# Four projection banks until the first scores, z:0 ahead of the first merge, and rk behind the second

## The chip, the cores and the metric

One core of a Trainium2 chip runs one launch of the kernel. The metric is the device time of the launch in microseconds (us). Engines: PE is TensorE, ACT ScalarE, DVE VectorE, POOL GpSimd, and SP is SyncE, whose queue issues every DMA of this kernel.

## The reference

Two post-norm decoder layers on a 256 x 1024 residual stream, float32. Each has one input projection for two head groups, an output projection, a norm, a gated MLP with a short convolution, and a second norm.

```python
def hybrid_layer(x, ...):
    proj = x @ w_in
    q_a, k_a, v_a, a_logit, b_logit, z, q_b, k_b, v_b = jnp.split(proj, offs, -1)
    o_a = gdn_mixer(q_a, k_a, v_a, a_logit, b_logit, z, ...)
    o_b = moba_mixer(q_b, k_b, v_b, pos)
    mix = jnp.concatenate([o_a, o_b], -1) @ w_out
    x = layer_norm(DEEPNORM_ALPHA * x + mix, ln1_g, ln1_b)
    ...
```

`gdn_mixer` is a gated delta rule with 4 heads of 128 and chunks of 64: q, k and v pass a causal convolution of four taps and silu, q and k are normalised, and for each chunk a unit lower triangular system (64 x 64, `a_strict` plus identity) is solved; its output is multiplied by silu(z). `moba_mixer` is block attention with 8 heads of 64; with 256 tokens it is one causal block.

## The kernel before, in words

Sequence is on the free axis: a projection chunk gives 128 output features x 256 tokens. A weight chunk is loaded in float32 by SP (`load_raw`, L181, tile wr, 6 buffers), split into a rounded part wh (ACT, L196) and a rest wl (DVE or POOL, L197), each in two halves of 512 columns and each in 5 buffers. `proj` (L204 to L214) then runs 24 matmuls of 128 x 256 into one PSUM bank: eight pairs xh·wh, xl·wh (L211, L212) and eight xh·wl (L214). The eight PSUM banks are divided (L94 to L96): pj has 2 (projections, by `ps_p`), mx 2 (scores, transposes, by `ps_m`) and ac 4 (by `ps_a`).

A layer has a mixing stage (about 20 to 160 us in layer 0, 368 to 506 us in layer 1) and an MLP stage, which the change does not touch. The mixing stage is written as units, `u_...`, that the tables `ORDER` (L72 to L87, one for a layer) list: `ka`, `va`, `qa` are the convolved projections of the delta rule (`u_conv`: projection, then ACT's L424 and DVE's three taps L427 read the bank, then tanh L429 and L430), `qb`, `kb` the rotary ones (`u_rope`), and `z` the gate (`u_z`: tanh L441 and zs L442 read the bank). `kk`, `decay`, `sk` and `am` make the triangular matrix A. `solve` inverts its 16 x 16 diagonal blocks on POOL: A goes to DRAM (da, L512), comes back as T (L518), DVE prepares it (L523), POOL runs 28 small steps (L527, L529) and a copy (L530), and the result goes to DRAM (dx, L531). `ex` reads it back (PT, L538) and DVE spreads it into gX and gx (L543). `lt` (L560) and `lx` merge 16 to 32, and `mt:32`, `mx:32`, `mt:64`, `mx:64` go on to 64. `s:p` makes attention scores of a head pair in two mx banks (L619, mask L623) and their softmax, `tr` and `pv` follow. `rk` is the inverse root of the key norms (some DVE operations on 128 x 8).

Order of work: letters behind @ in the table say on which engines the instructions of a unit are held behind those of the unit before (P is PE, A is ACT, D is DVE, G is POOL). Otherwise a scheduler places each engine's instructions by its own costs, and each engine then works them in that order. SP's queue is worked in order too: a DMA that waits holds back all behind it. In this queue the loads of layer 0's 16 weight chunks from ka:0 on stand between the masks and dx.

Of the kernel before, what the change touches and what calls it, by code (L numbers as in the profile page):

```python
# [22 lines left out]
D = 1024  # L23
S = 256
# [12 lines left out]
DP = 8 * (NB * 128 + NB)  # L37
# [33 lines left out]

ORDER = ("""  # L72
ab ka:0@A ab2@G ka:2@P qb:0@GP ka:3@G ka:1 kk:0 decay@AGD kk:1@PG kb:0@G kb:2@G sk@GP ld:0@P ld:1@DG kb:3@G am:0@A
vb:1@DAGP qb:1@GP kb:1@G rp@DG am:1@AG qb:2@G qb:3 va:2@GP va:0@G va:3 rk@G solve@G va:1@D qa:1 qa:0@P ex@DPA lt@GP s:0@DA lx@DAP
tr:0@AD mt:32:0@GAP mx:32:0@G mt:32:1@G vt:0@G rp@GP mx:32:1@PAG pv:0 mt:64:0@GDPA mt:64:1@AG s:1@AGD
qa:3@G qa:2@GP mx:64:0@PG tr:1@PA mx:64:1@D z:0 s:2@GADP pv:1@GA sq:0@DG vt:1@ADP zsol:0@D az tr:2@A s:3@GDP pv:2@AG
tr:3@PGD zsol:1@A z:2@G qk@GP sq:1@GDA o:0@ADP z:1@G wu:1@PGA pv:3@AGP o:1@GDP w:0:5 w:0:4@D w:1:4@PDA z:3@PD w:1:6@G
w:0:7@GD w:1:5@GPD ot:1@AP ot:0@G wu:0@PA w:0:6@A
""", """
vb:1@APDG ab@GD ka:0@G ab2@G ka:3 qb:0@P ka:2@G ka:1@P kk:0 decay@ADG kb:0 kk:1@GA kb:2 sk@AP kb:3@G kb:1@PG qb:2  # L80
rp@GPD qb:3@GP am:0@PA qb:1@DP am:1@AG ld:0@GP va:1@P va:0@GP rk@AG va:2@G ld:1@D solve@GP va:3@P qa:1 ex@D lt@DAP s:0@GD
lx@DAPG mt:32:0@A mt:32:1@AG vt:0@PD rp@GAD tr:0@AP qa:0 mx:32:0 pv:0@A mx:32:1@AD mt:64:0@AGD mt:64:1@DGP s:1@A
qa:3 qa:2@P mx:64:1@APD tr:1@P z:0@G s:2@G sq:0@D vt:1@DG mx:64:0@GDP pv:1 zsol:0@DGP az@A tr:2@DA s:3@GD pv:2@AG
tr:3@PDGA zsol:1@PD z:2 qk@PDG sq:1@G o:0@ADP z:1 pv:3@AGD o:1@A w:0:5@G w:0:4@DP w:1:4@GDA z:3@PA wu:0@DP w:1:6@GP
wu:1@GA w:0:7@D ot:1@D ot:0@AP w:1:5 w:0:6@PA
""")
# [3 lines left out]
def hybrid_kernel(ctx, tc, xT, x, wab, wch, par, lnrow, cst, msk, out):  # L90
# [10 lines left out]
    mx = ctx.enter_context(tc.tile_pool(name="mx", bufs=2, space=PSUM))  # L101
# [11 lines left out]
    def ps_p():  # L113
        return ps_w()[:, 0:S]

    def ps_w():
        return pj.tile([128, 512], F32, name="pj")

    def ps_m():
        return mx.tile([128, 512], F32, name="mx")  # L120
# [85 lines left out]
    def proj(ps, l, ci, le=None):  # L206
        h, lo = load_chunk(l, ci, le=le)
        h = h.rearrange("p (k m) -> p k m", k=KT)
        lo = lo.rearrange("p (k m) -> p k m", k=KT)
        for k in range(KT):  # L210
            pe.matmul(ps, h[:, k, :], xh[:, k, :], start=k == 0, stop=False)  # L211
            pe.matmul(ps, h[:, k, :], xl[:, k, :], start=False, stop=False)  # L212
        for k in range(KT):
            pe.matmul(ps, lo[:, k, :], xh[:, k, :], start=False, stop=k == KT - 1)  # L214
# [80 lines left out]
    def vb_first():  # L295
        vb = res.tile([128, 2, 512], F32, name="vb")
        ps = [ps_m() for _ in range(2)]
        for c in range(4):
            raw = wraw.tile([128, 1024], F32, name="wr")
            tiles = None  # L300
            for k in (range(2 * c, 2 * c + 2) if c == 0 else [slice(2 * c, 2 * c + 2)]):
                ks = slice(k, k + 1) if c == 0 else k
                load_x(ks)
                cs = slice(ks.start * 512 - c * 1024, ks.stop * 512 - c * 1024)
                sp.dma_start(raw[:, cs], wch[0, C_VB + c, :, cs])
                tiles = split(raw, tiles=tiles, cs=cs)
                wh, wl = tiles
                for t in range(2):
                    ts = slice(t * 128, t * 128 + 128)
                    for a, w in ((xh, wh), (xl, wh), (xh, wl)):  # L310
                        for kk in range(ks.start, ks.stop):
                            o = (kk - 2 * c) * 512
                            pe.matmul(ps[t], a[:, kk, ts], w[:, o:o + 512], start=kk == 0 and a is xh and w is wh,  # L313
                                      stop=kk == KT - 1 and w is wl)
        for t in range(2):
            act.activation(vb[:, t, :], ps[t], AF.Copy)
        return vb
# [20 lines left out]
    vb = vb_first()  # L338
    const_prep()

    for l in range(DEPTH):
# [7 lines left out]
        def sm(name):  # L349
            return small.tile(sh, F32, name=name, bufs=1)  # L350

        def mt(name, shape, bufs=1, dt=F32):
            return (early if name in EARLY else mix).tile(shape, dt, name=name, bufs=bufs)
# [5 lines left out]
        sk, cj, ncj, rk, sq, so, wv = (sm(n) for n in ("sk", "cj", "ncj", "rk", "sq", "so", "wv"))  # L359
        g_h = small.tile(sh, F32R, name="g_h", bufs=1)  # L360
        g_l = small.tile(sh, F32R, name="g_l", bufs=1)
        ka, qa = mt("ka", [128, HG, S]), mt("qa", [128, HG, S])
# [3 lines left out]
        qb, kb = mt("qb", [128, 4, S]), mt("kb", [128, 4, S])  # L366
# [8 lines left out]
        G, T, st = [], {}, {}  # L375
# [45 lines left out]
        def gdn_conv(ps, ct, dst):  # L421
            w = pr[:, P_GCONV + 4 * ct:P_GCONV + 4 * ct + 4]
            cv = mt("cv", [128, S], 2)
            act.activation(cv, ps, AF.Copy, scale=w[:, 3:4])  # L424
            for j in (2, 1, 0):
                o = 3 - j
                dve.scalar_tensor_tensor(cv[:, o:], ps[:, :S - o], w[:, j:j + 1], cv[:, o:], op0=OP.mult, op1=OP.add)  # L427
            th = mt("th", [128, S], 2)
            act.activation(th, cv, AF.Tanh, scale=0.5)  # L429
            dve.scalar_tensor_tensor(dst, th, 1.0, cv, op0=OP.add, op1=OP.mult)  # L430

        def u_conv(c0, ct, dst, h):
            ps = ps_p()
            proj(ps, l, c0 + h)
            gdn_conv(ps, ct + h, dst[:, h, :])

        def u_z(h):
            ps = ps_p()
            proj(ps, l, C_Z + h)
            th = mt("th", [128, S], 2)  # L440
            act.activation(th, ps, AF.Tanh, scale=0.5)  # L441
            dve.scalar_tensor_tensor(zs[:, h, :], th, 1.0, ps, op0=OP.add, op1=OP.mult)  # L442

        def u_rope(c0, dst, p):
            ps = ps_p()
            proj(ps, l, c0 + p)
            act.activation(dst[:, p, :], ps, AF.Copy)
            sw = mt("sw", [128, S], N_SW)
            dve.stream_shuffle(sw, dst[:, p, :], [(i + 8) % 16 if i < 16 else i for i in range(32)])
            dve.tensor_tensor(dst[:, p, :], dst[:, p, :], ropec, op=OP.mult)  # L450
            st["rp"] = st.get("rp", []) + [(dst, p, sw)]
# [158 lines left out]
                    dve.tensor_copy(X[hi, b, :, 0:n], ps[hi])  # L610

        def u_s(p):
            sc = [ps_m() for _ in range(2)]
            mxv = small.tile([128, 4], F32, name="mxv")
            for js, ks in ((slice(0, 128), slice(0, 128)), (slice(128, 384), slice(0, S))):
                for a in range(2):
                    rs = slice(64 * a, 64 * a + 64)
                    qs = slice(js.start, js.start + 128)
                    pe.matmul(sc[a][:, js], qb[rs, p, qs], kb[rs, p, ks], start=js.start == 0, stop=False,  # L619
                              skip_group_check=True)  # L620
            for a in range(2):
                for i in (0, 256):
                    pe.matmul(sc[a][:, i:i + 128], ident_b, neg_lt, start=False, stop=i > 0, skip_group_check=True)  # L623
            for a in range(2):
                dve.tensor_reduce(mxv[:, a:a + 1], sc[a][:, 0:128], axis=AX.X, op=OP.max)
                dve.tensor_reduce(mxv[:, 2 + a:3 + a], sc[a][:, 128:384], axis=AX.X, op=OP.max)
            dve.tensor_scalar(mxv, mxv, -(DH ** -0.5), None, op0=OP.mult)
            P = [mt("P0", [128, 2, 128], 2), mt("P1", [128, 2, S], 2)]
            sv = small.tile([128, 4], F32, name="sv")
            for i, js in enumerate((slice(0, 128), slice(128, 384))):  # L630
                for a in range(2):
                    c = 2 * i + a
                    act.activation(P[i][:, a, :], sc[a][:, js], AF.Exp, scale=DH ** -0.5, bias=mxv[:, c:c + 1],
                                   accum_out=sv[:, c:c + 1])
            rv = small.tile([128, 4], F32, name="rv")
            dve.reciprocal(rv, sv)
            for i in range(2):
                for a in range(2):
                    c = 2 * i + a
                    dve.tensor_scalar(P[i][:, a, :], P[i][:, a, :], rv[:, c:c + 1], None, op0=OP.mult)  # L640
            st["P", p] = P
# [132 lines left out]
        def u_ka(h):  # L774
            u_conv(C_KA, 4, ka, h)

        def u_va(h):
            u_conv(C_VA, 8, vz("va"), h)

        def u_qa(h):  # L780
            u_conv(C_QA, 0, qa, h)
# [103 lines left out]
        for j in range(2, FJ):  # L885
            cs = []
            for gi in range(2):
                ps = ps_p() if j > 2 or gi else head
# [14 lines left out]
        if l < DEPTH - 1:  # L903
            vb, vb_step = vb_start(l + 1)
# [99 lines left out]
```

## Time and profile before

| | us |
|---|---|
| three runs | 713.3, 714.86, 716.22 (median 714.86) |
| profiled execution, its time | 714.04 |
| its span | 712.3 |
| PE busy | 688.6 (97%) |
| DVE busy | 576.9 (81%) |
| ACT busy | 400.8 (56%) |
| POOL busy | 197.2 (28%) |
| mean granted PE clock | 0.984 |

The span is the time from the first to the last instruction of the profiled execution, 1.7 us less than its own time. Times of rows are counted from the start of the span. Ends of matmuls are modelled and overlap, so their rate is read from start to start.

### The profile page before, as it was taken

The page shows a single profiled execution, that of the slowest core. Times are in us where ns is not written, and L with a number is a line of the kernel's source. Part 1 is how long each engine was busy: PE and PEld are TensorE (multiplying, and loading weights), DVE is VectorE, ACT ScalarE, POOL GpSimd, SP SyncE. Part 2 cuts the span into 40 slices and gives each one's busy share as a digit, 9 for nine tenths or more (in the row PEclk, how much of TensorE's full clock was granted, in tenths as well). Part 3 has the DMA queues.
Part 4 walks back from the last instruction along what each step waited for, and adds up shares of the span by engine and source line. Part 5 has one row for each costly group of instructions (what it writes and reads, how often), then busy time and mean ns, then how long its engine had stood idle before and what let it go on. Part 6 is the DMA issues. An engine that isn't in the chain of part 4 may idle for free.

```text
span 712.3 us, 13664 instructions
## 1 busy us (share of the span) xinstructions
PE 688.6 (97%) x5056; PEld 618.6 (87%) x5056; DVE 576.9 (81%) x1273; ACT 400.8 (56%) x908; POOL 197.2 (28%) x200
## 2 busy tenths in 40 slices
PE   8989999999999999999999989999999999999994
PEld 5979888787999999999888988888789999999994
DVE  5899877599788887778879987776998888887756
ACT  5644466546666665656355445556476566666531
POOL 0045700013333343332002382000153333333413
PEclk9999999999999999999999997999999999999998
DMA  8876351521766665656153437134246766666201
GB/s 313 305 244 192 78 198 40 199 89 61 276 220 194 211 222 184 202 181 205 60 201 129 144 94 222 61 103 159 66 150 234 233 213 194 214 206 202 70 1 60
DMA packets 41217, 118.07 MB, mean 166 GB/s; under 512 B 10176, under 2 KB 12992, under 8 KB 40640
## 3 DMA queue, kind: packets, MB, share of 16 engines
q1 hardware_dynamic: 41152, 117.21, 49.6%
q8 instruction: 40, 0.66, 0.3%
q14 instruction: 25, 0.20, 0.1%
HBM read 114.84 MB, written 2.36 MB: 165 GB/s over the span
## 4 chain that ended last, share of the span: by engine, by line
PE 86%; DVE 9%; ACT 1%; issue 1%; DMA 1%; SPq 0%; DVEq 0%; ACTq 0%
PE pj L211 16%; PE pj L212 15%; PE pj L214 15%; PE ac L732 8%; PE ac L733 8%; PE ac L734 8%; DVE wl L197 3%; PE pj L225 1%; PE pj L222 1%; DVE cv L427 1%; PE mx L619 1%; PE pj L223 1%; PE mx L313 1%; DMA wr<-in_wch_dram 1%; PE mx L662 1%
## 5 line engine op out<-in xcount | busy, mean ns | idle before, releaser
L196 ACT ACTIVATE wh<-wr 128x512 fp32r<-128x512 f32 x376 | 219.5, 622 | 108.2 <-PE pj L212 49.1
L211 PE MATMUL pj<-xh,wh 128*128 128x256 f32 x1024 | 258.6, 289 | 7.4 <-DVE cv L427 7.4
L212 PE MATMUL pj<-xl,wh 128*128 128x256 f32 x1024 | 257.2, 287 | 0.0
L197 DVE TENSOR_TENSOR wl<-wr,wh 128x512 fp32r<-128x512 f32 x292 | 206.7, 736 | 28.2 <-ACT wh L196 14.7
L211 PEld LDWEIGHTS pj<-xh,wh 128*128 128x128 f32 x1024 | 198.6, 194 | 11.4 <-issue 5.4
L212 PEld LDWEIGHTS pj<-xl,wh 128*128 128x128 f32 x1024 | 199.1, 194 | 1.6
L197 POOL TENSOR_TENSOR wl<-wr,wh 128x512 fp32r<-128x512 f32 x84 | 116.2, 1405 | 204.9 <-ACT wh L196 199.7
L214 PE MATMUL pj<-xh,wl 128*128 128x256 f32 x1024 | 147.6, 286 | 0.0
L214 PEld LDWEIGHTS pj<-xh,wl 128*128 128x128 f32 x1024 | 134.2, 194 | 0.4 <-issue 0.2
L733 PE MATMUL ac<-wh,fal 128*128 128x512 f32 x144 | 56.4, 392 | 0.0
L732 PE MATMUL ac<-wh,fah 128*128 128x512 f32 x144 | 56.1, 392 | 0.0
L734 PE MATMUL ac<-wl,fah 128*128 128x512 f32 x144 | 56.0, 389 | 0.0
L842 DVE TENSOR_TENSOR fal<-fth,fah 128x256 fp32r<-128x256 f32 (+1 forms) x48 | 36.8, 767 | 17.3 <-ACT fah L841 17.0
L828 DVE SCALAR_TENSOR_TENSOR fc<-pj,par,fc 128x255 f32<-128x255 f32 x80 | 38.1, 476 | 4.2 <-ACT fc L824 2.8
L828 DVE SCALAR_TENSOR_TENSOR fc<-pj,hw,fc 128x255 f32<-128x255 f32 x80 | 38.3, 478 | 3.7 <-ACT fc L824 2.4
L817 POOL TENSOR_SCALAR hw<-par 128x66 f32<-128x66 f32 x2 | 2.1, 1048 | 139.2 <-DVE wlh L197 139.2
L839 DVE SCALAR_TENSOR_TENSOR fth<-fth,fc 128x256 f32<-128x256 f32 (+1 forms) x48 | 23.6, 492 | 20.1 <-ACT fth L838 20.1
L841 ACT ACTIVATE fah<-fth 128x256 fp32r<-128x256 f32 (+1 forms) x48 | 18.9, 393 | 34.8 <-DVE fth L840 34.8
L838 ACT ACTIVATE fth<-fc 128x256 f32<-128x256 f32 (+1 forms) x48 | 19.2, 400 | 31.7 <-DVE fc L828 31.5
L427 DVE SCALAR_TENSOR_TENSOR cv<-pj,par,cv 128x255 f32<-128x255 f32 (+2 forms) x72 | 33.8, 472 | 0.6 <-ACT cv L424 0.3
L734 PEld LDWEIGHTS ac<-wl,fah 128*128 128x128 f32 x144 | 27.1, 188 | 5.9
L732 PEld LDWEIGHTS ac<-wh,fah 128*128 128x128 f32 x144 | 27.1, 189 | 4.8
(257 smaller groups left out, 1030.5 us busy)
## 6 DMA issues: line engine op xcount, KB each, us to landing
wr<-in_wch_dram SPq DMA_DIRECT2D x195, 512.0 KB, 4.1
lnb<-in_lnrow_dram SPq DMA_DIRECT2D x4, 1024.0 KB, 4.6
xres<-in_x_dram SPq DMA_DIRECT2D x2, 512.0 KB, 6.8
da<-A SPq DMA_DIRECT2D x4, 256.0 KB, 3.4
ka<-in_wch_dram SPq DMA_DIRECT2D x2, 512.0 KB, 4.5
qa<-in_wch_dram SPq DMA_DIRECT2D x2, 512.0 KB, 5.1
qb<-in_wch_dram SPq DMA_DIRECT2D x2, 512.0 KB, 4.8
kb<-in_wch_dram SPq DMA_DIRECT2D x2, 512.0 KB, 5.7
```

The costliest lines, as they stand in the source:

```text
L196: ih = act.activation(h[:, s], raw[:, s], AF.Copy)
L197: il = le.tensor_tensor(lo[:, s], raw[:, s], h[:, s].bitcast(F32), op=OP.subtract)
L211: pe.matmul(ps, h[:, k, :], xh[:, k, :], start=k == 0, stop=False)
L212: pe.matmul(ps, h[:, k, :], xl[:, k, :], start=False, stop=False)
L214: pe.matmul(ps, lo[:, k, :], xh[:, k, :], start=False, stop=k == KT - 1)
L427: dve.scalar_tensor_tensor(cv[:, o:], ps[:, :S - o], w[:, j:j + 1], cv[:, o:], op0=OP.mult, op1=OP.add)
L732: pe.matmul(ps, a_h, w_h[:, ns], start=start and i == 0, stop=False, skip_group_check=True)
L733: pe.matmul(ps, a_l, w_h[:, ns], start=False, stop=False, skip_group_check=True)
L734: pe.matmul(ps, a_h, w_l[:, ns], start=False, stop=stop and i == len(items) - 1, skip_group_check=True)
L828: dve.scalar_tensor_tensor(cv[:, d], ps[:, d.start - o:d.stop - o], w[:, q:q + 1], cv[:, d], op0=OP.mult, op1=OP.add)
L839: dve.scalar_tensor_tensor(th, th, 1.0, cg[:, ts], op0=OP.add, op1=OP.mult)
L842: dve.tensor_tensor(al, th, ah.bitcast(F32), op=OP.subtract)
```

## The change

Until the first `s` unit of a layer is written, every second projection of `u_conv`, `u_z` and `u_rope` takes a bank of mx in place of one of pj, so that four banks take turns. `z:0` moves from behind `mx:64` to a place ahead of `ex`, and `rk` from ahead of the solve to a place behind `mx:32:0` (layer 0) or `mt:32:0` (layer 1), without letters. The new function stands at L432, so the lines behind it are 4 further down than before, from `u_s` on 5.

```diff
-vb:1@DAGP qb:1@GP kb:1@G rp@DG am:1@AG qb:2@G qb:3 va:2@GP va:0@G va:3 rk@G solve@G va:1@D qa:1 qa:0@P ex@DPA lt@GP s:0@DA lx@DAP
-tr:0@AD mt:32:0@GAP mx:32:0@G mt:32:1@G vt:0@G rp@GP mx:32:1@PAG pv:0 mt:64:0@GDPA mt:64:1@AG s:1@AGD
-qa:3@G qa:2@GP mx:64:0@PG tr:1@PA mx:64:1@D z:0 s:2@GADP pv:1@GA sq:0@DG vt:1@ADP zsol:0@D az tr:2@A s:3@GDP pv:2@AG
+vb:1@DAGP qb:1@GP kb:1@G rp@DG am:1@AG qb:2@G qb:3 va:2@GP va:0@G va:3 solve@G va:1@D qa:1 qa:0@P z:0 ex@DPA lt@GP s:0@DA lx@DAP
+tr:0@AD mt:32:0@GAP mx:32:0@G rk mt:32:1@G vt:0@G rp@GP mx:32:1@PAG pv:0 mt:64:0@GDPA mt:64:1@AG s:1@AGD
+qa:3@G qa:2@GP mx:64:0@PG tr:1@PA mx:64:1@D s:2@GADP pv:1@GA sq:0@DG vt:1@ADP zsol:0@D az tr:2@A s:3@GDP pv:2@AG
...
-rp@GPD qb:3@GP am:0@PA qb:1@DP am:1@AG ld:0@GP va:1@P va:0@GP rk@AG va:2@G ld:1@D solve@GP va:3@P qa:1 ex@D lt@DAP s:0@GD
-lx@DAPG mt:32:0@A mt:32:1@AG vt:0@PD rp@GAD tr:0@AP qa:0 mx:32:0 pv:0@A mx:32:1@AD mt:64:0@AGD mt:64:1@DGP s:1@A
-qa:3 qa:2@P mx:64:1@APD tr:1@P z:0@G s:2@G sq:0@D vt:1@DG mx:64:0@GDP pv:1 zsol:0@DGP az@A tr:2@DA s:3@GD pv:2@AG
+rp@GPD qb:3@GP am:0@PA qb:1@DP am:1@AG ld:0@GP va:1@P va:0@GP va:2@G ld:1@D solve@GP va:3@P qa:1 z:0 ex@D lt@DAP s:0@GD
+lx@DAPG mt:32:0@A rk mt:32:1@AG vt:0@PD rp@GAD tr:0@AP qa:0 mx:32:0 pv:0@A mx:32:1@AD mt:64:0@AGD mt:64:1@DGP s:1@A
+qa:3 qa:2@P mx:64:1@APD tr:1@P s:2@G sq:0@D vt:1@DG mx:64:0@GDP pv:1 zsol:0@DGP az@A tr:2@DA s:3@GD pv:2@AG
...
+        def ps_q():
+            st["proj"] = st.get("proj", 0) + 1
+            return ps_m()[:, 0:S] if st["proj"] % 2 and "s" not in st else ps_p()
+
...
-            ps = ps_p()
+            ps = ps_q()
...
         def u_s(p):
+            st["s"] = True
             sc = [ps_m() for _ in range(2)]
```

(The third of the last pieces stands alike in `u_conv`, `u_z` and `u_rope`.)

What this moves is seen in each engine's order of the built programs; the names are those of the program, with a number where a name is used again.

SP's queue in layer 0, from the last loads ahead of A's way to DRAM to the first load behind dx. Before:

```order
L292 DMA lnb<-in_lnrow_dram 128x2048
L181 DMA wr<-in_wch_dram 128x1024 x2
L145 DMA par_4532<-in_par_dram 128x265
L379 DMA abr<-in_wab_dram 128x64
L512 DMA da<-A_245 128x4x128
L512 DMA da<-A_246 128x4x128
L181 DMA wr<-in_wch_dram 128x1024 x2
L518 DMA T<-da 64x16x16
L181 DMA wr<-in_wch_dram 128x1024 x4
L531 DMA dx<-P_983 64x2x256
L181 DMA wr<-in_wch_dram 128x1024
L538 DMA PT_1140<-dx 128x16x16
```

And after:

```order
L292 DMA lnb<-in_lnrow_dram 128x2048
L181 DMA wr<-in_wch_dram 128x1024 x5
L145 DMA par_4532<-in_par_dram 128x265
L379 DMA abr<-in_wab_dram 128x64
L516 DMA da<-A_245 128x4x128
L516 DMA da<-A_246 128x4x128
L181 DMA wr<-in_wch_dram 128x1024 x2
L522 DMA T<-da 64x16x16
L181 DMA wr<-in_wch_dram 128x1024 x3
L535 DMA dx<-P_972 64x2x256
L181 DMA wr<-in_wch_dram 128x1024
L542 DMA PT_1165<-dx 128x16x16
```

Of the loads between T and dx one has moved ahead of da (two more have moved from the other side of lnb). The single load behind dx is a chunk of w_out, as before; in layer 1 it is that of z:1, as before.

DVE and ACT in layer 0, ahead of the first merge: first DVE, from the third tap of qa:1 (before) and from the second tap of qa:0 (after) to the end of `ex`. Before:

```order
L427 SCALAR_TENSOR_TENSOR cv<-pj,par_216,cv 128x253
L197 TENSOR_TENSOR wl<-wr,wh 128x512
L430 SCALAR_TENSOR_TENSOR qa<-th,cv 128x256
L427 SCALAR_TENSOR_TENSOR cv<-pj,par_216,cv 128x255
L197 TENSOR_TENSOR wl<-wr,wh 128x512
L427 SCALAR_TENSOR_TENSOR cv<-pj,par_216,cv 128x254
L427 SCALAR_TENSOR_TENSOR cv<-pj,par_216,cv 128x253
L430 SCALAR_TENSOR_TENSOR qa<-th,cv 128x256
L543 TENSOR_TENSOR gX<-PT_1140,kt 128x256
L543 TENSOR_TENSOR gx<-PT_1140,kt 128x512
```

After:

```order
L427 SCALAR_TENSOR_TENSOR cv<-pj,par_216,cv 128x254
L197 TENSOR_TENSOR wl<-wr,wh 128x512
L427 SCALAR_TENSOR_TENSOR cv<-pj,par_216,cv 128x253
L197 TENSOR_TENSOR wl<-wr,wh 128x512
L430 SCALAR_TENSOR_TENSOR qa<-th,cv 128x256
L446 SCALAR_TENSOR_TENSOR zs<-th,mx 128x256
L547 TENSOR_TENSOR gX<-PT_1165,kt 128x256
L547 TENSOR_TENSOR gx<-PT_1165,kt 128x512
```

And ACT, after, up to the copy that follows the first merge:

```order
L196 ACTIVATE wh<-wr 128x512 x2
L424 ACTIVATE cv<-pj,par_216 128x256
L429 ACTIVATE th<-cv 128x256
L196 ACTIVATE wh<-wr 128x512 x2
L429 ACTIVATE th<-cv 128x256
L445 ACTIVATE th<-mx 128x256
L196 ACTIVATE wh<-wr 128x512 x2
L565 ACTIVATE T_1173<-ac 128x256
```

The two wl, and the second pair of wh, are those of the w_out chunk whose load stands behind dx; z:0's tanh and zs follow them, and gX follows zs. In layer 1 the same rows stand ahead of gX, with the chunk of z:1 in the place of that of w_out.

PE in layer 0, around the first merge. Before:

```order
L211 MATMUL pj<-xh,wh 128x256
L560 MATMUL ac<-gX,A_245 64x32 x8
L212 MATMUL pj<-xl,wh 128x256
L211 MATMUL pj<-xh,wh 128x256
L212 MATMUL pj<-xl,wh 128x256
L211 MATMUL pj<-xh,wh 128x256
L212 MATMUL pj<-xl,wh 128x256
L560 MATMUL ac<-gX,A_246 64x32 x8
```

After, with the scores' second mx bank (rows of L624 and L628) at the merge:

```order
L212 MATMUL pj<-xl,wh 128x256
L624 MATMUL mx<-kb,qb 128x128
L564 MATMUL ac<-gX,A_245 64x32 x8
L624 MATMUL mx<-kb,qb 128x256
L628 LDWEIGHTS ident_b
L628 MATMUL mx<-neg_lt,ident_b 128x128
L628 LDWEIGHTS ident_b
L628 MATMUL mx<-neg_lt,ident_b 128x128
L564 MATMUL ac<-gX,A_246 64x32 x8
L214 MATMUL pj<-xh,wl 128x256 x4
```

The first row after is the 16th matmul of qa:3; counted from qa:1's first, 88 projection matmuls stand ahead of the merge, before it was 79. The scores' second bank is the one that z:0's projection had. In layer 1 the scores stand ahead of the merge as a whole, and 28 projection matmuls stand between the end of qa:1 and the merge, where 31 stood before.

## Rows read from the trace of the kernel before

**Rows 1.** The page, busy us of PE (share of the span).

```profile
PE 688.6 (97%) x5056; PEld 618.6 (87%) x5056; DVE 576.9 (81%) x1273; ACT 400.8 (56%) x908; POOL 197.2 (28%) x200
```

**Rows 2.** TensorE's waits: us in total, times, longest.

```profile
PE pj L211 <- DVE cv L427: 7.4, 6, 2.1
```

**Rows 3.** TensorE's timeline: start, us, instruction, [idle before and what ended it].

```profile
39.20 0.36 PE L211 MATMUL pj<-xh,wh 128*128 128x256 f32 x1 [1.37 <-DVE cv L427]
...
68.73 0.28 PE L212 MATMUL pj<-xl,wh 128*128 128x256 f32 x1
68.85 1.12 PE L214 MATMUL pj<-xh,wl 128*128 128x256 f32 x8
72.05 0.43 PE L211 MATMUL pj<-xh,wh 128*128 128x256 f32 x1 [2.08 <-DVE cv L427]
...
82.94 0.70 PE L619 MATMUL mx<-kb,qb 64*128 64x256 f32 x2
...
419.14 0.36 PE L211 MATMUL pj<-xh,wh 128*128 128x256 f32 x1 [2.04 <-DVE cv L427]
...
435.45 0.36 PE L211 MATMUL pj<-xh,wh 128*128 128x256 f32 x1 [1.48 <-DVE cv L427]
```

**Rows 4.** Windows: length, busy PE PEld DVE ACT POOL, PEclk, DMA share, GB/s.

```profile
28.00:74.00 46.00, 42.08 (x318) 39.92 (x318) 45.76 (x128) 22.65 (x49) 22.32 (x24) 0.98 0.70 233
74.00:91.00 17.00, 17.00 (x129) 15.82 (x129) 13.38 (x28) 8.61 (x19) 11.26 (x25) 0.95 0.39 98
...
392.00:404.00 12.00, 12.00 (x93) 11.47 (x92) 10.56 (x40) 5.20 (x12) 4.67 (x6) 1.00 0.34 116
...
72.20:75.50 3.30, 3.30 (x17) 3.30 (x18) 2.59 (x6) 0.57 (x2) 2.75 (x8) 0.50 0.10 42
420.40:423.70 3.30, 3.30 (x18) 3.08 (x16) 1.50 (x3) 1.16 (x3) 2.67 (x9) 0.50 0.02 5
437.50:447.60 10.10, 10.10 (x142) 9.48 (x142) 6.65 (x22) 4.97 (x17) 0.00 (x0) 0.50 0.65 243
```

**Rows 5.** TensorE's timeline at the first merge of layers 0 and 1.

```profile
91.45 0.66 PE L560 MATMUL ac<-gX,A 64*64 64x32 f32 x16
...
95.75 1.22 PE L214 MATMUL pj<-xh,wl 128*128 128x256 f32 x8
...
436.66 0.66 PE L560 MATMUL ac<-gX,A 64*64 64x32 f32 x16
...
443.16 2.07 PE L214 MATMUL pj<-xh,wl 128*128 128x256 f32 x8
```

**Rows 6.** SyncE's queue, and DMA issues with KB and median us to landing.

```profile
82.88 0.60 SPq L531 DMA_DIRECT2D dx<-P  x1
83.61 0.52 SPq L181 DMA_DIRECT2D wr<-in_wch_dram  x1
85.32 0.38 SPq L538 DMA_DIRECT2D PT<-dx  x1
...
430.59 0.55 SPq L181 DMA_DIRECT2D wr<-in_wch_dram  x1
...
wr<-in_wch_dram SPq DMA_DIRECT2D x195, 512.0 KB, 4.1
...
PT<-dx SPq DMA_DIRECT2D x2, 128.0 KB, 3.3
```

**Rows 7.** ScalarE's timeline ahead of the first merges.

```profile
86.84 0.40 ACT L429 ACTIVATE th<-cv 128x256 f32<-128x256 f32 x1
...
434.43 0.63 ACT L196 ACTIVATE wh<-wr 128x512 fp32r<-128x512 f32 x1 [3.44 <-DMA wr<-in_wch_dram]
```

**Rows 8.** VectorE's timeline ahead of layer 0's first merge.

```profile
87.74 0.48 DVE L427 SCALAR_TENSOR_TENSOR cv<-pj,par,cv 128x255 f32<-128x255 f32 x1
88.14 0.68 DVE L197 TENSOR_TENSOR wl<-wr,wh 128x512 fp32r<-128x512 f32 x1
...
90.98 0.42 DVE L543 TENSOR_TENSOR gX<-PT,kt 128x256 f32<-128x256 f32 x1
```

More of the change, by code (lines that the diff above doesn't have):

```diff
@@ L437, in u_z @@
         def u_z(h):
-            ps = ps_p()
+            ps = ps_q()
             proj(ps, l, C_Z + h)
@@ L444, in u_rope @@
         def u_rope(c0, dst, p):
-            ps = ps_p()
+            ps = ps_q()
             proj(ps, l, c0 + p)
```

## Prediction

> **What bounds the kernel now.** I read the page's busy shares first, then TensorE's waits, then the timeline around each of them, then the windows with the granted clock, and last the queues that feed the first merge. TensorE is busy 688.6 of 712.3 us [rows 1], so only its 23.7 us of idleness and its time at half clock can be won, and any microsecond that it stands still is lost. The largest wait is for a projection bank: 7.4 us in six pieces, all in front of a projection's first matmul, released by VectorE's convolution L427 [rows 2]. The larger four are 1.37, 2.08, 2.04 and 1.48 us [rows 3]. That is what four banks aim at.
>
> The second thing to see is what follows. The first merge (u_lt, L560) starts at 91.45 us in layer 0 and 436.66 us in layer 1 [rows 5], and it needs the solved 16x16 blocks. These come down one chain: GpSimd's solve, dx to DRAM at 82.88, PT back at 85.32, on SyncE's queue, which is worked in order [rows 6]. VectorE, which makes A for this chain, is busy 45.76 of the 46.00 us from 28 to 74 us [rows 4]: no free bank makes that part shorter. So a wait removed before the merge is worth something only if TensorE has other work until the merge can start.
>
> **Clock.** The granted clock is 0.50 in three stretches [rows 4]: behind the waits of 2.08 and 2.04 us for about 3.3 us each, and behind that of 1.48 us, with the merge's small matmuls following, for 10.1 us. Layer 0's first merge ran at full clock: there eight third-pass matmuls take 1.22 us, in layer 1's low stretch 2.07 us [rows 5]. That is 0.85/2.07, or 41% of the time spent low: 1.4 us for a 3.3 us stretch, at most 4.1 us for the long one.
>
> **The change, part by part.**
>
> Banks. In layer 0 the projections va:3, va:1, qa:1, qa:0, z:0 can now run back to back behind va:0, whose last eight matmuls start at 68.85, one per 0.12 us [rows 3]. va:0 is issued by 69.81; five projections of 24 x 0.12 = 2.88 us give 84.2; four score matmuls add 0.7, as two took at 82.94 [rows 3], and 16 of qa:3 1.9 us: TensorE stands in front of the second half of the scores at about 86.8, up to 1.4 us sooner with the wait at 39.20 gone too. VectorE's weight differences may hold it back on the way; nothing in the sum depends on it.
>
> z:0 ahead of the merge. By the built order the merge waits for gX (L547), which on VectorE stands behind zs (L446); in layer 0 the scores' second bank waits for zs too. Zs waits for ScalarE's tanh, and that stands behind two copies of a weight chunk (a w_out chunk in layer 0, z:1 in layer 1) whose load is queued on SyncE behind dx. Before, one copy of that chunk and none of its wl stood ahead of gX. So the start of the merge is now: load landed, then 0.63 (copy) + 0.68 (wl) + 0.48 (last tap of qa) + 0.40 (its tanh) + 0.40 (tanh of z) + 0.42 (zs, taken as gX, which has its shape) + 0.42 (gX) = 3.4 us [rows 7, 8].
>
> Layer 0: one more weight load is ahead of da, and an issue takes 0.52 us [rows 6], so T, the solve and dx come 0.5 us later (at most; nothing if the queue had slack). Load issued 83.61 + 0.5, landed 4.1 us later, 88.2, plus 3.4: merge at 91.6, against 91.45. Lower end: were only PT binding, 85.32 + 0.5 + 3.3 = 89.1 plus gX, 89.6. Upper end: a load a microsecond slower, 92.6. I take 91.6, since every step of it has a row. Nine more projection matmuls (88 instead of 79, counted from qa:1) are then done, 9 x 0.12 = 1.08, and the scores' second bank, some 0.4 us, is still to do: 0.7 us of TensorE's work ahead. Layer 0: +0.15 - 0.7 = **-0.5 us**. TensorE then waits in one piece for 91 - 86.8, over 4 us, where it had 2.08 us.
>
> Layer 1: VectorE is idle 1.4 of the 12 us from 392 to 404 [rows 4], and with banks free most of this goes: A, T and dx some 1.2 us sooner (0 to 1.4). The chunk of z:1, issued at 430.59, was copied at 434.43 after 3.44 us of ScalarE's waiting for its DMA [rows 6, 7]; now 433.2, plus 3.4, merge at 436.6, against 436.66. Three projection matmuls fewer are done by then: **+0.3 us** (-0.4 to +1.5).
>
> Clock. Layer 0's merge now stands behind a wait of over 4 us, twice what set the clock low before. The row nearest to it is layer 1's: same small matmuls, clock 0.50 for 10.1 us. Ends: 1.4 us lost (one short stretch) and 4.1 us (the long one). I take the middle, **+2.7 us**, as part of the low time can fall on the wait itself. The two short stretches of before lay ahead of the merge, where TensorE now waits anyway: their end is worth nothing. Layer 1's merge was at half clock already: 0, with -1 to +1.5.
>
> The norms' inverse root. Its dozen operations on eight elements barely move in the built order, still ahead of the solve's first multiplication on VectorE, because rk has no order letters any more and nothing holds it back: 0. Were it to move behind mx:32:0, VectorE would gain some tenths of a microsecond ahead of the solve.
>
> Later filler: z:0 is missing behind the merges, but qa:3 and qa:2 come there; TensorE's total of matmuls is unchanged and it had no waits of note there: 0, with 0.5 us either way.
>
> Sum: -0.5 + 0.3 + 2.7 = +2.5 us against the profiled execution's 714.04: **716.5 us**. The three runs' median is 714.86; I add nothing for the 0.8 us between them, which is inside the runs' own spread of 713.3 to 716.22.
>
> **Rivals.**
>
> *The waits go and the time with them.* All of the 7.4 us and the two short low stretches, 2.8 us, come off: 703.8 us. For it: the wait is the largest that TensorE has. The Trainium skill, "Perfetto Trace Analysis", Matmul Optimizations, says the same, that all 8 PSUM banks should be used; no run here shows it yet. Against it: the merge's date is set by the solve's chain, and TensorE would need 7 us of work that the order gives it only after the merge. Chance 0.12.
>
> *The clock holds.* TensorE is held back by VectorE on its way, so the waits stay in small pieces and layer 0's merge runs at full clock as before: the sum without +2.7, 713.8 us. For it: VectorE had 13.38 us of work in the 17 us before the merge [rows 4]. Chance 0.15.
>
> *Half clock outlasts the merge (slower).* The two waits, now above 4 us each, keep the clock at 0.50 for a stretch longer in both layers, into mt:32 and the projections around it. Each further stretch of 3.3 us costs 1.4 us: 716.5 + 2.8 = 719.3 us, one more 720.7. It decides from two further stretches on. For it: 1.48 us were enough for 10.1 us [rows 3, 4]. Against it: the clock came back there while the merge's matmuls still ran. The Trainium skill, same page and section, warns that the matmul engine's power follows its use and wants matmuls back to back in batches; by that rule one long wait is the worse exchange, and the trace's three low stretches, each behind a wait, agree. Chance 0.26.
>
> **How the numbers follow.** My forecast has 0.47, with a range of its own of 714 to 718.6 us. A difference under 0.5% (3.6 us, 711.3 to 718.4) can't be told from no change here. Forecast: same 0.37, slower 0.08, faster 0.02. Clock holds: same 0.105, faster 0.045. Waits pay: faster 0.12. Half clock lasts: slower 0.19, same 0.07. Together faster 0.18, same 0.55, slower 0.27. The range of 8 in 10 leaves out the paying rival and the far end of the last: 711 to 720.5 us.
>
> **What would show it.** Right: the wait on L427 near zero; in its place, in both layers, a wait of 4 us or more in front of L624 (its second bank) or L564, ended by VectorE's zs or gX; ScalarE waiting for the DMA of a weight chunk just ahead of z:0's tanh; the merge within 1 us of 91.5 and of 436.6; granted clock 0.5 behind 91 us in layer 0. Wrong: a merge at 89 us or sooner, a clock of 1.0 throughout it, or bank waits that merely move.

## The result, and the profile after

The changed kernel takes 725.16 us (median of 4 runs, 723.27 to 726.2) where the kernel before takes 714.62 us (4 runs on the same chips): a ratio of 1.0135, 95% interval 1.0106 to 1.0165. It is slower, by 10.5 us, and outside the range that was given. The profiled execution's span is 723.8 us against 712.3, 11.5 us more.

The page of the changed kernel, TensorE's busy time and the granted clock in 40 slices:

```profile
PE 691.8 (96%) x5056; PEld 620.6 (86%) x5056; DVE 576.3 (80%) x1273; ACT 401.3 (55%) x908; POOL 198.6 (27%) x200
...
PEclk9999969999999999999999996899999999999998
```

Idle time has gone from 23.7 us to 723.8 - 691.8 = 32.0 us, and the same 5056 matmuls are busy 3.2 us longer [rows 1]; the two slices with a 6 show why: the clock is low around both first merges. TensorE's waits answer to [rows 2]:

```profile
PE mx L624 <- DVE zs L446: 4.8, 1, 4.8
PE ac L564 <- DVE gX L547: 4.5, 1, 4.5
PE mx L624 <- DVE cv L427: 2.9, 2, 1.8
```

The 7.4 us in front of L211 are gone, as they were meant to be. In their place stand 12.2 us: the scores' banks (L624), which the projections now hold and of which 2.9 us still end with VectorE's L427, and the merge (L564). TensorE's timeline of the changed kernel at these places answers to [rows 3, 5]:

```profile
85.19 0.89 PE L624 MATMUL mx<-kb,qb 64*128 64x128 f32 x4 [1.77 <-DVE cv L427]
...
93.03 0.79 PE L624 MATMUL mx<-kb,qb 64*128 64x128 f32 x2 [4.76 <-DVE zs L446]
93.75 1.06 PE L564 MATMUL ac<-gX,A 64*64 64x32 f32 x16
...
446.20 1.07 PE L564 MATMUL ac<-gX,A 64*64 64x32 f32 x16 [4.51 <-DVE gX L547]
```

In layer 0 the merge waits behind zs, and zs behind a weight load. SyncE's queue, then ScalarE, then VectorE of the changed kernel, as against [rows 6 to 8]:

```profile
85.42 0.60 SPq L535 DMA_DIRECT2D dx<-P  x1
86.15 0.51 SPq L181 DMA_DIRECT2D wr<-in_wch_dram  x1
87.85 0.38 SPq L542 DMA_DIRECT2D PT<-dx  x1
```

```profile
89.93 1.15 ACT L196 ACTIVATE wh<-wr 128x512 fp32r<-128x512 f32 x2 [4.43 <-DMA wr<-in_wch_dram]
91.77 0.42 ACT L429 ACTIVATE th<-cv 128x256 f32<-128x256 f32 x1 [0.69 <-DVE cv L427]
92.09 0.36 ACT L445 ACTIVATE th<-mx 128x256 f32<-128x256 f32 x1
```

```profile
90.59 0.69 DVE L197 TENSOR_TENSOR wl<-wr,wh 128x512 fp32r<-128x512 f32 x1 [1.15 <-ACT wh L196]
...
92.56 0.41 DVE L446 SCALAR_TENSOR_TENSOR zs<-th,mx 128x256 f32<-128x256 f32 x1
92.89 0.42 DVE L547 TENSOR_TENSOR gX<-PT,kt 128x256 f32<-128x256 f32 x1
```

Read from the top: dx leaves at 85.42, the load behind it at 86.15, ScalarE gets the chunk after 4.43 us of waiting, and from its copy at 89.93 to the merge's first ready operand, gX at 92.89 plus 0.42, 3.38 us pass. The sum of the prediction had 3.4. PT, issued at 87.85, landed 3.4 us later, at 91.3: the load holds gX back some 1.6 us longer than PT does.

Windows from the merge's first matmul to that of mt:32, layer 0 and layer 1. Before (columns as in [rows 4]):

```profile
91.45:99.22 7.77, 7.60 (x162) 6.84 (x162) 7.24 (x22) 5.00 (x18) 0.00 (x0) 1.00 0.71 273
436.66:448.19 11.53, 11.53 (x162) 10.74 (x162) 8.08 (x24) 5.00 (x18) 0.00 (x0) 0.56 0.65 241
```

And after:

```profile
93.75:106.16 12.41, 12.41 (x166) 10.94 (x165) 5.60 (x18) 5.35 (x18) 0.00 (x0) 0.55 0.55 211
446.20:458.21 12.01, 12.01 (x165) 11.20 (x165) 6.48 (x19) 4.58 (x16) 0.00 (x0) 0.57 0.53 209
...
91.40:104.90 13.50, 11.87 (x157) 10.35 (x157) 7.45 (x22) 5.38 (x18) 0.00 (x0) 0.50 0.60 231
439.60:456.50 16.90, 12.39 (x162) 10.89 (x161) 6.77 (x21) 5.32 (x19) 2.07 (x4) 0.50 0.72 234
```

With nearly the same number of matmuls, layer 0's stretch went from 7.77 us at clock 1.00 to 12.41 us at 0.55. Layer 1's was slow already, at 0.56. The last two rows span the time at a granted clock of 0.50 around each merge: 13.5 and 16.9 us, where there were 10.1 in layer 1 alone, besides two stretches of 3.3 ahead of the merges [rows 4].

Where the 11.5 us are is read from the first instruction of a line in each trace (before, after, us between the two marks; layer 1 is counted from the first L225 of its v projection):

| from, to | layer 0 | layer 1 |
|---|---|---|
| start of the layer, DVE's first step of the solve | 64.72, 66.45 | 48.30, 47.54 |
| that step, first merge | 26.73, 27.30 | 24.97, 26.49 |
| first merge, mt:32 | 7.77, 12.40 | 11.52, 12.01 |
| mt:32, first activations of the MLP | 69.26, 71.02 | 72.18, 71.73 |
| these, end of the layer | 194.91, 195.00 | 191.93, 193.86 |

Layer 0 gives +1.73 +0.57 +4.63 +1.76 +0.09 = 8.8, layer 1 -0.76 +1.52 +0.49 -0.45 +1.93 = 2.7. The first entry is mostly scatter: with dx on GpSimd's queue, which changes no order up to there, the kernel before reached that step at 66.13 us and the changed one at 64.98. So is a part of the second row: where layer 0's order is that of before, it takes 25.9 to 28.4 us (before, and the kernels of experiments 6, 8, 9 and 10 that leave it so).

### The profile page after: what moved, and what is told of

The parts are those of the page before. It is cut to its first block, busy times and chain, and to the rows that moved or that the text cites. A ratio compares the mean times of both kernels' runs of the same rounds, so it can differ in the third digit from the quotient of the medians.

```text
span 723.8 us, 13658 instructions
## 1 busy us (share of the span) xinstructions
PE 691.8 (96%) x5056; PEld 620.6 (86%) x5056; DVE 576.3 (80%) x1273; ACT 401.3 (55%) x908; POOL 198.6 (27%) x200
## 4 chain that ended last, share of the span: by engine, by line
PE 79%; DVE 9%; POOL 5%; DMA 3%; ACT 2%; issue 2%; SPq 0%; DVEq 0%; ACTq 0%; POOLq 0%
PE pj L211 13%; PE pj L214 13%; PE pj L212 13%; PE ac L738 7%; PE ac L737 7%; PE ac L739 7%; DVE wl L197 3%; POOL P L533 2%; DMA wr<-in_wch_dram 2%; POOL T L531 2%; PE mx L624 1%; PE pj L225 1%; ACT wh L196 1%; PE mx L313 1%; PE pj L222 1%
## 5 line engine op out<-in xcount | busy, mean ns | idle before, releaser
L211 PE MATMUL pj<-xh,wh 128*128 128x256 f32 x872 | 219.8, 288 | 0.2 <-DVE fc L833 0.2
L212 PE MATMUL pj<-xl,wh 128*128 128x256 f32 x872 | 218.5, 287 | 0.0
L211 PEld LDWEIGHTS pj<-xh,wh 128*128 128x128 f32 x872 | 169.7, 195 | 2.4 <-issue 0.6
L212 PEld LDWEIGHTS pj<-xl,wh 128*128 128x128 f32 x872 | 169.5, 194 | 1.5
L214 PE MATMUL pj<-xh,wl 128*128 128x256 f32 x872 | 126.8, 287 | 0.0
L214 PEld LDWEIGHTS pj<-xh,wl 128*128 128x128 f32 x872 | 114.7, 194 | 0.3
L211 PE MATMUL mx<-xh,wh 128*128 128x256 f32 x152 | 38.2, 287 | 0.0
L212 PE MATMUL mx<-xl,wh 128*128 128x256 f32 x152 | 37.7, 285 | 0.0
```

## The experiments

Theory A: the banks themselves cost, since they let weight differences pass A on VectorE. Theory B: the banks are harmless and z:0 costs, by its tie to a load behind dx. Beside either, theory C: half clock behind the longer wait is the largest part.

**1. Banks alone.** The changed kernel with both tables of before.

```diff
-... va:3 solve@G va:1@D qa:1 qa:0@P z:0 ex@DPA ... mx:32:0@G rk mt:32:1@G
+... va:3 rk@G solve@G va:1@D qa:1 qa:0@P ex@DPA ... mx:32:0@G mt:32:1@G
```

> Only the four banks; the order tables as before. Theory A (the banks cost: with free banks VectorE's order takes more weight differences ahead of A, so A, T and the merge come later in layer 0, and TensorE, with its projections done early, waits longer in front of the merge and goes to half clock): slower than before by 5 to 9 us, 720 to 724 us, merge of layer 0 at 92.5 us or later, a wait of 3 us or more ahead of it. Theory B (the banks are harmless and z:0 costs, by its tie to a weight load behind dx): within 2 us of before, 713 to 717 us, merge at about 91 us.

715.5 us, ratio 1.0014 (0.9997 to 1.003): no difference. The merge of layer 0 starts at 90.69 us and A's last operation at 55.21 against 55.18, so theory A falls. Nothing is won either: TensorE waits 4.5 us for gX in layer 1 and 3.3 us for the scores' banks. The wait has moved.

**2. Order alone.** The new tables, two banks.

```diff
-            return ps_m()[:, 0:S] if st["proj"] % 2 and "s" not in st else ps_p()
+            return ps_p()
```

> Only the order of z:0 and rk; two projection banks as before. Theory A: within 3 us of before, 714 to 718 us, since A comes as early as before and the waits for banks stay spread. Theory B: slower by 7 us or more, 722 to 726 us, with the merge of layer 0 behind zs at 92 us or later and a wait of 4 us ahead of it.

719.7 us, ratio 1.0055 (1.0021 to 1.009), between the two theories: with the merge of layer 0 at 93.63 us, 29.28 us behind the solve's first step (before 26.73). Its runs lie between 714.0 and 723.61 us, and the mean clock goes with them: 714.0 at 0.992, 723.61 at 0.981. The profiled one took 715.08 us, at full clock through both merges (8.11 and 7.93 us to mt:32), so its trace does not hold the 5 us. And what holds the merge back in it is not theory B's tie:

```profile
82.73 3.29 DVE L197 TENSOR_TENSOR wl<-wr,wh 128x512 fp32r<-128x512 f32 x1
...
90.46 1.15 ACT L196 ACTIVATE wh<-wr 128x512 fp32r<-128x512 f32 x2 [1.46 <-PE pj L212]
```

ScalarE's copy of the chunk behind dx waits here for TensorE, not for the load. TensorE had waited 1.95 us at 88.27 for a bank that VectorE's taps released, and ahead of these taps stands a weight difference of 3.29 us, where others of that shape take 0.7. It ran beside four operations of GpSimd (L455, L456). Alone the two parts add 1 and 5 us, together 10.5.

**3. Zeros behind z:0.** Sixteen matmuls of zeros added in each layer.

```diff
+        def u_wm():
+            ps = ps_a()
+            for _ in range((16, 16)[l]):
+                pe.matmul(ps, zero_t[:, 0:128], zero_t, start=True, stop=True)
...
-... z:0 ex@DPA ...
+... z:0 wm@P ex@DPA ...
```

> The changed kernel with 16 matmuls of zeros (128x512) in a bank of their own behind z:0 in both layers, that fill part of TensorE's wait ahead of the merge and compute nothing that is used. Theory C (half clock behind the long wait is a large part of the loss): granted clock 1.0 or a much shorter low stretch at the merge, 4 to 6 us faster than the changed kernel, 719 to 721 us. Theory D (the late merge and the filler lost are the loss, the clock a small part): within 2 us of the changed kernel's 725.

725.43 us, the changed kernel's time, and the clock as low as there. But it tells nothing: the scheduler put the scores and 16 matmuls of qa:3 behind the merge, the zeros ran right after z:0 (82.75 to 86.4 us in layer 0), and waits of 6.28 and 5.68 us were left ahead of the two merges.

**4. dx on GpSimd's queue.** No other instruction of any engine moves; SyncE's weight load no longer stands behind dx.

```diff
-            dma.dma_start(dap(dx, 0, ...
+            pool.dma_start(dap(dx, 0, ...
```

> The changed kernel with dx issued on GpSimd's queue, so that SyncE's queue lets the next weight load pass ahead of it; nothing else in any engine's order differs. If zs and gX wait for that load (theory B's tie): zs and gX 2 to 3 us sooner unless PT binds, merge of layer 0 at about 91.5 to 92 us instead of 93.75, total 721 to 723 us. If PT or A's date binds: merge within 0.7 us of 93.75, total within 1.5 us of 725; a DMA that is slow to start on GpSimd's queue would make it later.

721.2 us, ratio to before 1.0103 (1.0061 to 1.0145), 4 us below the changed kernel (four runs of each, 720.19 to 723.29 and 723.27 to 726.2). VectorE ahead of layer 0's merge in this run:

```profile
88.51 0.41 DVE L446 SCALAR_TENSOR_TENSOR zs<-th,mx 128x256 f32<-128x256 f32 x1
89.73 0.42 DVE L547 TENSOR_TENSOR gX<-PT,kt 128x256 f32<-128x256 f32 x1 [0.81 <-DMA PT<-dx]
```

zs comes 4 us sooner than in the changed kernel, and gX waits for PT, as it should. From the solve's first step to the merge it is 25.23 us in place of 27.30. (That step itself came at 64.98 us here and at 66.45 in the changed kernel's trace, with the same order: the 1.5 us are scatter of the start.) The solve is not what differs: PT landed 24.7 us behind that step here (issued at 86.81, 2.9 us to land) and 24.8 in the changed kernel. So the tie is shown and costs some 2 us at this merge. In layer 1 it is 25.34 us in place of 26.49, some 1.1 us more. TensorE still waits 2.18 and 0.75 us at layer 0's merge, and the clock still falls: 11.83 us to mt:32.

The queue changed one thing more than the load. In the changed kernel a weight difference of VectorE took 3.36 us from 85.36 on, beside GpSimd's L459 and L460; here, where GpSimd issues dx first, none at this place took over 0.84 us. In the changed kernel it was not on the path, as ScalarE waited for the load until after its end.

**5. Zeros through the whole wait.** As 3, with 40 and 38 of them.

> The changed kernel with 40 (layer 0) and 38 (layer 1) matmuls of zeros behind z:0, enough to keep TensorE busy through the whole wait until the merge can start; they compute nothing that is used. The scores and 16 matmuls of qa:3 move behind the merge, which costs about 0.7 + 1.9 us a layer. If half clock is the larger part of the loss (4.6 us from the merge to mt:32 in layer 0, some 4 in layer 1): granted clock 1.0 through both merges, merge to mt:32 at about 10 us in place of 12.4, total 718 to 722 us. If the clock is not the point: total 727 us or more, by the filler that the zeros push behind the merge.

721.73 us (717.61 to 726.53), ratio 1.0077 (1.0044 to 1.0111), where the changed kernel had 1.0135. In the profiled execution the two layers came out apart:

```profile
92.54 0.65 PE L565 MATMUL ac<-gX,A 64*64 64x32 f32 x16 [1.20 <-DVE gX L548]
...
445.72 0.66 PE L565 MATMUL ac<-gX,A 64*64 64x32 f32 x16 [2.06 <-DVE gX L548]
```

```profile
92.54:104.63 12.09, 11.81 (x169) 10.52 (x169) 4.41 (x15) 4.20 (x16) 0.00 (x0) 0.58 0.55 224
445.72:453.52 7.80, 7.52 (x167) 6.72 (x168) 5.19 (x17) 3.97 (x15) 0.00 (x0) 1.00 0.81 319
```

Layer 1's merge ran at full clock, 7.80 us against the changed kernel's 12.01 with as many matmuls; in layer 0 the clock fell, and nearly the same matmuls took 12.09 us. So the clock is worth over 4 us at a merge. The waits left ahead of the merges do not tell the two apart: 1.20 us stood where the clock fell and 2.06 us where it held. What the zeros push behind layer 1's merge costs most of the gain again, 75.40 us from mt:32 to the first activations against 71.73. The four runs at a mean clock of 0.996 took 717.6 to 718.8 us, the one at 0.983 took 726.5. Theory C holds as far as this: half clock is the largest single part. The changed kernel, at a mean clock of 0.974 to 0.978 in its four runs, pays it at both merges of its trace, the kernel before at layer 1's alone, so the change adds the price of one merge.

**6. Zeros in the kernel before.** Six behind qa:1 in layer 1; and, in another kernel, eight between va:0 and va:3 in layer 0.

```diff
-... qa:1 ex@D lt@DAP ...
+... qa:1 wm:6@P ex@D lt@DAP ...
```

> The kernel before with six matmuls of zeros behind qa:1 in layer 1 alone (1.4 us of TensorE's wait of 1.48 us ahead of the merge there). If a wait of 1.5 us in front of the merge is what sets the clock low: layer 1's merge at clock 1.0, from merge to mt:32 7.5 to 9 us in place of 11.5, total 710 to 712 us. If the low clock comes from the merge's small matmuls themselves, or from what went before: low stretch of 10 us stays, total 714 to 716 us.

717.73 us, ratio 1.0025 (1.0002 to 1.0047). Six more matmuls changed the scheduler's order around the merge, a wait of 1.8 us for gX stood there, and the clock fell there for part of the merge; 10.78 us to mt:32. A miss: the zeros did not reach the wait that counts.

> The kernel before with eight matmuls of zeros between va:0 and va:3 in layer 0, most of the wait of 2.08 us there. If that wait sets the clock low: no low stretch at 72 to 76 us. The time gains at most 1.4 us by it (713 to 714), and nothing if TensorE then only waits longer for the merge; anything beyond that would come from elsewhere.

716.7 us, ratio 1.0008 (0.9982 to 1.0033). The low stretch at 72 us is gone and the time is not better: TensorE waits 0.83 and 1.70 us for banks later on in layer 0 and 1.47 us for gX in layer 1, and other low stretches came (one through layer 1's merge, 12.3 us to mt:32). No gain from the clock ahead of the merge is seen, as other waits take its place.

**7. Order alone, dx on GpSimd's queue.** Experiments 2 and 4 together.

> Only the order of z:0 and rk (two banks), with dx on GpSimd's queue. If z:0's cost is its tie to the weight load behind dx: layer 0's merge at 91.5 us or sooner in place of 93.6, total 714 to 717 us with less scatter from run to run. If z:0's cost is the filler that is missing at the end of the mixing stage (ScalarE's oh, norms): total stays at 718 us or more, and the stretch from mt:32 to the first activations of the MLP stays at 70.9 us in layer 0 against 69.3.

715.05 us, ratio 0.9993 (0.9961 to 1.0025): the 5 us of experiment 2 are gone, the merge starts at 90.44 us in place of 93.63. The scatter is not: 711.54 us at a clock of 0.995, 719.9 at 0.986. From mt:32 to the first activations layer 0 still takes 70.95 us. That part belongs to z:0's move itself. What the queue took away here is not shown to be the tie, since experiment 2's trace did not wait for the load at this merge; the weight difference of 3.29 us is gone too, and from 82 us to gX the longest of its shape takes 1.04 us.

**8. The same queue in the kernel before, and with the banks.**

(The e8 of the text is experiment 7.)

> The kernel before with dx on GpSimd's queue and nothing else. There one copy of the weight chunk behind dx stands ahead of gX, so if that tie is what the queue costs: merge at most 1 us sooner, total 713 to 715 us. If GpSimd's queue itself brought e8's gain: 711 to 713 us.

713.72 us, ratio 0.9973 (0.9942 to 1.0004): 1.2 us less, not clear of the noise.

> The four banks alone, with dx on GpSimd's queue. The banks' wait ahead of layer 1's merge (4.5 us) ends with gX behind PT, which dx's queue hardly moves: half clock at layer 1's merge stays, total 714 to 716 us. If the banks' cost were that tie too: 711 to 713 us.

716.06 us, ratio 1.0012 (0.9991 to 1.0033). Without z:0 ahead of it, the queue changes little; the banks gain nothing by it.

**9. z:0 and rk moved in layer 1 alone, two banks, dx on GpSimd's queue.**

> Two banks; the new order of z:0 and rk in layer 1 alone; dx on GpSimd's queue. If z:0's move costs its filler at the end of the mixing stage in layer 0 alone (70.9 against 69.3 us from mt:32 to the first activations) and brings layer 1's merge at full clock (7.9 us to mt:32 in place of 11.5): 709 to 712 us, the fastest so far. If the clock at layer 1's merge falls as it likes from run to run: 712 to 716 us.

711.75 us, ratio 0.9951 (0.9927 to 0.9975): faster than both kernels, by 0.5% against the one before. In its trace layer 1's merge ran at full clock, 8.28 us to mt:32.

**10. The same with dx on SyncE's queue.**

> As the run before, with dx on SyncE's queue as in the kernel before. If z:0's tie to the load behind dx costs in layer 1 too (zs and gX behind the copy of z:1): 1 to 3 us above the run with dx on GpSimd's queue. If the tie costs in layer 0 alone: the same within 1 us.

716.36 us, ratio 1.0011 (0.9981 to 1.0041), 4.6 us above experiment 9, from which only dx's queue differs (in both layers). The two profiled executions, of 712.21 and 717.89 us, reach the solve's first step in layer 1 at the same moment, 413.9 us. The end of GpSimd's solve and TensorE from there, experiment 9:

```profile
430.78 0.63 POOL L530 COPY P<-P 64x256 f32<-64x256 f32 x1
...
438.26 0.66 PE L560 MATMUL ac<-gX,A 64*64 64x32 f32 x16
...
446.54 0.59 PE L596 MATMUL ac<-gX,A 32*32 32x32 f32 x16 [0.38 <-DVE gX L586]
```

And experiment 10:

```profile
432.05 0.79 POOL L530 COPY P<-P 64x256 f32<-64x256 f32 x1
...
440.06 1.05 PE L560 MATMUL ac<-gX,A 64*64 64x32 f32 x16 [1.95 <-DVE gX L543]
...
452.03 0.59 PE L596 MATMUL ac<-gX,A 32*32 32x32 f32 x16
```

ScalarE of experiment 10 shows the load that it waits for:

```profile
437.42 1.15 ACT L196 ACTIVATE wh<-wr 128x512 fp32r<-128x512 f32 x2 [5.72 <-DMA wr<-in_wch_dram]
```

The merge comes 1.80 us later, but not by the tie alone. GpSimd's last step ends 1.43 us later (432.84 against 431.41), before this layer's dx is issued in either run, so its queue has no part in that: in experiment 9 the clock had fallen at 422.1 for 3.4 us, VectorE's work came 1.5 us later, and GpSimd's steps beside it were shorter. The tie's own part is what gX waits beyond PT: PT, issued at 435.29, took 3.1 us to land, and gX at 439.59 stands 1.2 us behind that; in experiment 9 it stands 0.4 us behind PT's landing. Behind the wait of 1.95 us the clock takes another 11.97 - 8.28 = 3.7 us to mt:32. So the pair shows a small wait and a larger price behind it; how much of the 4.6 us between the medians the tie brings in layer 1 is not separated from the rest that dx's queue does, in layer 0 too.

## Why the prediction was wrong

Its picture of the path held. The waits on L427 in front of L211 went and nothing was won by it; the merge's date is set by the solve's chain and, now, by the weight load; the new waits are those that were named, 4.76 and 4.51 us where "4 us or more" stood; the copy-to-merge chain measured 3.38 us for 3.4; rk hardly moved (in layer 1 it stands one place later, behind the solve's first multiplication). The rival in which the waits pay (703.8 us) falls with experiment 1. For that rival the prediction had the Trainium skill ("Perfetto Trace Analysis", Matmul Optimizations), which asks that all 8 PSUM banks be used. The kernel before used all eight already, divided 2, 2 and 4, so this does not speak for the rival. The run with the banks alone shows no gain from giving projections four of them, since the wait moves to gX (4.5 us in layer 1).

What failed is the sum, above all in two terms: the clock at layer 0's merge and the filler that was put at nothing.

"Clock, **+2.7 us**" measured +4.63 in layer 0, above even the upper end of 4.1. I took the middle, on the ground that part of the low time would fall on the wait. It did, 2.35 us of it, but the low stretch was longer than the row it was taken from: 13.5 us in layer 0, where 10.1 stood at layer 1's merge before. That left 11.15 us behind the merge's start, and 41% of this is the 4.6. That is the mechanism of the third rival, half clock that outlasts the merge. It had 0.26, and it is the case that came. It put a further stretch into both layers; in layer 1 the low stretch grew to 16.9 us, but from the merge to mt:32 that cost 0.49 us. The same page and section of the Trainium skill asks for matmuls back to back in batches, and between the two traces it agrees: 7.77 us without the long wait, 12.41 behind it, for nearly the same work. In experiment 5, though, a wait of 2.06 us left the clock at 1.00.

"Later filler: 0, with 0.5 us either way" measured +1.76 in layer 0. z:0 was work for TensorE at the end of the mixing stage, where the output of the delta rule comes last. Without it the output projection stands and waits:

```profile
157.29 0.50 PE L737 MATMUL ac<-wh,oh 128*128 128x512 f32 x1 [1.43 <-ACT oh L727]
```

All six kernels with z:0 moved in layer 0 (the changed one, experiments 2, 3, 4, 5 and 7) have 70.9 to 71.2 us from mt:32 to the first activations; the eight without have 69.3. That the matmuls' total is unchanged was no reason for 0: it is where they stand that counts. With this goes the "- 0.7" for TensorE's work done ahead of the merge: the stretch behind mt:32 has 510 matmuls in place of 520, as that term had it, and is longer all the same.

"Layer 0: +0.15" for the merge's date measured +0.57 behind the solve's first step, and that step came 1.73 us later in this execution. Most of the latter is scatter, and the +0.57 is within it. So the merges came at 93.75 and 446.20 us, neither within 1 us of its forecast, though layer 1's, seen from the start of its layer, was only 0.76 us late.

Layer 1: "A, T and dx some 1.2 us sooner" did not come. The solve's first step was 0.76 us sooner behind the start of the layer, but GpSimd's solve took 19.2 us from that step in place of 18.2, so dx, at 438.96 (429.90 before), left 0.3 us later behind the start of the layer than before. Why the solve took longer was not tried. The mixing stage of layer 1 was foretold at +0.3 and measured +0.80.

The MLP of layer 1 was not in the sum and measured +1.93. One wait of it is seen:

```profile
531.83 0.50 PE L222 MATMUL pj<-whh,xh 128*128 128x512 f32 x1 [0.79 <-ACT xh L280]
```

In the built order of the changed kernel the first activations' transposes stand behind four of the eight that make xh for the second tile, before behind six; experiment 4 has the same order and 193.46 us for this part. That this order is the cause was not tried, and another trace speaks against its being all of it: the banks with dx on GpSimd's queue (experiment 8) took 193.6 us with all eight ahead, experiment 1 with that same order 192.1. It stays open.

Two parts that cost 1 and 5 us alone cost 10.5 us together. The likely reason is the clock, but it is argued and not shown: banks let TensorE run to the merge early, the tie holds the merge back, so the wait is the sum of both and the clock is low at both merges, where each part alone left at least one of the two at full clock in its profiled execution. The mean clocks go with it: 0.974 to 0.978 in the four runs of the changed kernel, 0.981 to 0.988 with the banks alone, 0.981 to 0.992 with the order alone.

## What to carry to other kernels

A wait that is taken away from an engine that must then wait for something else is only moved, and many short waits that become one long one can cost more than all of them, if half clock comes behind it. Before a unit is pulled forward, list what its small operations stand behind on every engine, down to the DMA queue: here a gate's multiplication was tied to a load that stood behind a DMA waiting for another engine. And when work is taken from a place, ask what that place still has to do while its own last result arrives. Two traces that differ by one edit can differ by chance as well: look where they first part, and whether the edit can have reached that point.

## What was not expected of the hardware

The granted clock is not the same in two executions of one kernel, and the time follows it: experiment 2 took 714.0 to 715.1 us at a mean clock of 0.992 and 723.6 at 0.981, experiment 5 took 717.6 us at 0.996 and 726.5 at 0.983, some 0.7 to 0.9 us for each 0.001. In experiment 10 a wait of 1.95 us stood ahead of a merge at half clock; in experiment 7 one of 2.3 us left the clock at 1.00, and experiment 5 has both within one execution. So the length of the wait alone does not tell.

A weight difference of VectorE that takes 0.7 us elsewhere took 3.3 to 3.4 us in several traces (3.36 in the changed kernel, 3.29 in experiment 2) beside GpSimd's L455 and L456 (L459 and L460 in the changed kernel), and reads as busy all the time.

A DMA issued on GpSimd's queue took it 0.83 us (layer 0 of experiment 4) and landed in 2.5 us (median), on SyncE's queue 0.60 and 2.4: a queue that is free at the right moment cost almost nothing more.
